# w_down loaded in whole rows, and the last expert group worked expert by expert, in a decoder block with a mixture of experts

## The chip, the core and the metric

The kernel runs on one core of a Trainium2 chip. Such a core has a matrix engine (PE in the profile, with its weight loads listed apart as PEld), a vector engine (DVE), a scalar engine (ACT), a general engine (POOL) and a sequencer that does nothing here but issue transfers (SP). Weights come from HBM, the chip's memory, through 16 DMA engines into SBUF; PE writes its sums to PSUM. The metric is the device time of one execution in microseconds (us), lower is better. Times inside a profile are counted from the start of its span, which runs from the first instruction to the last.

## The reference

One decoder block on 256 tokens of 1024 columns, all in float32: attention beside a convolution, cross-attention into a memory, and then the part that the change touches, a mixture of 32 experts and a last norm. A token picks one of 4 groups and two of its 8 experts. Cut to that:

```python
def hierarchical_moe(h, w_route_group, b_route_group, w_route_expert, b_route_expert, w_gate, w_up, w_down):
    t = h.reshape(-1, D)                                   # 256 x 1024
    ...                                                    # gates [32, 256]: two entries per token
    def expert_step(y, args):
        wg, wu, wd, ge = args                              # 1024x512, 1024x512, 512x1024
        out = (jax.nn.silu(t @ wg) * (t @ wu)) @ wd
        return y + ge[:, None] * out, None
    y, _ = lax.scan(expert_step, jnp.zeros_like(t), (w_gate, w_up, w_down, gates))

x = x + hierarchical_moe(rmsnorm(x, norm_ffn_g), ...)
return rmsnorm(x, final_g)
```

Each of `w_gate`, `w_up` and `w_down` is 2.1 MB per expert, so the 32 experts hold 201 of the 237 MB that the program moves.

## The kernel before, in words

The first third of the time goes to the norms, the attention, the convolution, the cross-attention and the routing. Then come the experts, in 8 groups of 4. An expert takes up to 32 tokens, so a group fills 128 slots. For one group:

- `gather` (L968) multiplies the tokens `X` by a matrix `SR` that picks and scales them, which gives `tg`, the tokens transposed, with the 32 slots of expert q in columns 32q to 32q+31.
- 32 products each for `eg` (gate) and `eu` (up) at L1151. Expert q uses only the 32 columns of PE that belong to it, so four experts stand side by side in the array; a product of float32 shows as two records in the trace. Each needs the weights of that expert.
- `hidden_T` (L985 to L992) makes silu(eg) * eu and transposes it into `hT`.
- 32 products `ed` (L1181) with `w_down`, in two column halves of 512, the four experts again side by side; ACT copies each half from PSUM to `yd` (L1000), and `combine` (L1002) adds it, weighted by the gates in `GST`, to the experts' sum `Y`, which stays in PSUM over all groups.

In the last group the columns come in slices of 512, 256, 128 and 128, and the products go expert after expert. Behind each slice `out_slice` adds the residual `X` (L1099), squares and sums on ACT (`fjunk`, L1102) and multiplies by the last gain (L1107); after the last slice the root (`fr`, L1104), its reciprocal (L1213), the scaling and four transfers to the output follow. ACT needs another table for the root; the kernel loads it ahead of time (L1192).

All weights go through one ring of slots of 1024 KB, called 1 MB here (1.0486 million bytes; class `Ring`). SP issues the loads in one fixed order, group by group: 8 loads of `w_gate`, 8 of `w_up`, 8 of `w_down`. A load waits until the slot that it takes has been read for the last time, and for the eighth transfer before it, since eight completion semaphores go round. `w_gate` and `w_up` are cut by rows: a partition's piece of a load is 4 rows of 512 floats that follow each other in memory, 8 KB. `w_down` is cut by columns: a partition's piece is 512 columns of each of its 4 rows, four runs of 2 KB; in the last group the runs are 2 KB, 1 KB and 512 bytes (`down_cols`). The last gain `final_g` is loaded by ACT's queue in the last group and takes its turn on those semaphores (L1163).

Of the kernel before, what the change touches and what calls it, by code (L numbers as in the profile page):

```python
# [16 lines left out]
OP = mybir.AluOpType  # L17
# [3 lines left out]
P = 128  # L21
# [37 lines left out]
class Ring:  # L59
    """Weight loads in a fixed order through slots of SBUF: a load starts as soon as a slot is free.  # L60
    Larger tensors of the first phase live in slots too, so that their memory joins as they end."""
# [25 lines left out]
    def spare(self, shape, dt=F32):  # L87
        """a slot for another tensor [P, *shape]: the tensor and the slot"""
# [9 lines left out]
    def queue(self, key, shape, src, within=None):  # L98
        """within: the load of an earlier key whose slot this one shares, and the columns there"""
        self.todo.append((key, shape, src, within))  # L100

    def pump(self, limit=1000):
        while self.todo and limit:
# [13 lines left out]
            # the very first in two parts, so that the arithmetic starts sooner  # L117
# [22 lines left out]
class Pair:  # L140
    """An operand [P, NJ, S] of 24 significant bits as two of 12; each half of its rows in one slot."""
# [16 lines left out]
def down_cols(g):  # L158
    """column slices of w_down's loads; finer at the end"""
    return [(0, 512), (512, 512)] if g < NE // 4 - 1 else [(0, 512), (512, 256), (768, 128), (896, 128)]  # L160


def body(tc, a, out):
# [55 lines left out]
    # U[s, t] = 1 where s <= t  # L219
# [3 lines left out]
    # the same in bf16, which holds 0 and 1 exactly  # L223
# [4 lines left out]
    # the tensor engine's clock rests when it idles: products nobody reads keep it up meanwhile  # L228
# [16 lines left out]
    # router columns: NG group columns, padding that never wins, NE expert columns  # L245
# [4 lines left out]
    # group of each expert column  # L250
# [18 lines left out]
    # the chunks of v and the forget gate are wider than the others  # L269
# [30 lines left out]
    for g in range(NE // 4):  # L300
# [5 lines left out]
        for n, (c0, w) in enumerate(down_cols(g)):  # L306
            for q in range(4):
                wv = w_down[4 * g + q].rearrange("(p j) n -> p j n", j=4)
                if n < 3:
                    ring.queue(("ed", g, n, q), (4, 256 if n == 2 else w), wv[:, :, c0:c0 + w])  # L310
                else:
                    ring.queue(None, (4, w), wv[:, :, c0:c0 + w], (("ed", g, 2, q), slice(128, 256)))
# [30 lines left out]
    def rsqrt(src, scale, shape, name, pool=None, out=None):  # L343
        """(src * scale + eps) ** -0.5, with one Newton step on the vector engine"""
# [17 lines left out]
    def ssq(ss, src, eng):  # L362
        """ss [P, 1] = sum of squares along src [P, n]"""
# [8 lines left out]
    def ssq_rstd(src, n, name):  # L372
        """src [P, NT, n] -> rstd [P, NT]"""
# [11 lines left out]
    def split(v):  # L385
        """hi + lo == v exactly, each of 12 significant bits; a few rows of v at a time"""
# [17 lines left out]
    def put_split(pair, j, src, g):  # L404
        """split (src * g) into pair[:, j]"""
# [3 lines left out]
    def transposed(pair, src, g, k0, k1, cols, name):  # L409
        """pair[:, k] = split of g[:, k] * (cols(k) of src)^T, for k in k0 .. k1"""  # L410
# [14 lines left out]
    def normed(src, dst):  # L425
        """rmsnorm, without the gain, of src [P, NT, D] into dst"""
# [11 lines left out]
    def wstat(key, pair, name):  # L438
        """256 columns of a projection, transposed: two [P, S] in PSUM"""
# [10 lines left out]
    def astat(key, pair, n, name, outs=None, first=True, last=True, j0=0, bank=mm_ps):  # L450
        """n columns of a projection, natural: NT tiles [P, n] in PSUM"""
# [85 lines left out]
    # log_sigmoid(f) = min(f, 0) - ln(1 + exp(-|f|)) and its cumulative sum  # L537
# [14 lines left out]
    def cum_2():  # L552
        """-c by head"""
# [6 lines left out]
    def cum_3():  # L560
        """-c the same in every partition: [masked block 0 | block 0 | masked block 1]"""
# [266 lines left out]
    def x_blocks(i, k0, k1):  # L828
        """tT[:, k] = gain * (columns of block k)^T for the tokens of tile i"""
# [24 lines left out]
    # the last products tile by tile, so that the first tile's steps run beside the second's  # L854
# [42 lines left out]
    # experts outside the token's group drop out  # L897
# [15 lines left out]
    # place of each token in its expert's list, from 1  # L913
# [20 lines left out]
    # the experts' sum, [NT][2] tiles [P, 512], grows in PSUM over all groups  # L934
    Yp = [[psY.tile([P, 512], F32, name="Y%d%d" % (i, n)) for n in range(2)] for i in range(NT)]

# [1 line left out]
    last_pick = [None]  # L938

    def pick_mats(key_v, n, eng, SR=None):  # L940
        """S picks tokens into slots; SR has 1/rms for its ones"""
# [11 lines left out]
    def gate_mats(Sv, g_v, n):  # L953
        """the gates in place of S's ones"""
# [291 lines left out]
```

## Time and profile before

| | before |
|---|---|
| time, median of 3 runs | 707.68 us (706.91 to 707.87) |
| span of the profiled execution | 705.3 us |
| PE busy | 583.4 us (83% of the span) |
| DVE, ACT, POOL busy | 32%, 25%, 17% |
| moved by DMA | 237.36 MB, 337 GB/s over the span |
| mean granted clock of PE | 0.971 of full speed |

The profile gives its execution by the span; the median of the runs is 2.4 us longer than it. A busy PE is not one at its peak, since its records overlap. From about 264 us on, the 16 DMA engines are busy without a break until about 692 us.

### The profile page before, as it was taken

How to read it: one execution, taken by the hardware profiler on the slowest of the kernel's cores; microseconds unless marked ns; L12 is line 12 of the kernel's file. 1: busy time of each engine (PE TensorE's matmuls, PEld its weight loads, DVE VectorE, ACT ScalarE, POOL GpSimd, SP SyncE). 2: the span in 40 equal slices, each digit the busy share in tenths (PEclk: the TensorE clock that was granted, in tenths of full speed). 3: DMA queues.
4: the chain of work that ended last, by engine and by line, in shares of the span. 5: the costliest groups of instructions: out<-in, count | busy, mean ns of one | idle time of the engine just before them, and what ended most of it. 6: DMA issues, size and time to landing. Idle time of an engine off the chain costs nothing. (4 is left out here: it accounts for less than half of the span.)

```text
span 705.3 us, 8963 instructions
## 1 busy us (share of the span) xinstructions
PE 583.4 (83%) x3517; PEld 344.8 (49%) x3517; DVE 224.2 (32%) x496; ACT 175.0 (25%) x384; POOL 122.1 (17%) x106
## 2 busy tenths in 40 slices
PE   7999999899899999998657856866796787679685
PEld 4999889678897752525112511511251151125124
DVE  5799789785765620401000100100010010001013
ACT  6474765484444600010000000000000000000023
POOL 5556435493434100000000000000000000000000
PEclk9999999999999999999999999998998999999898
DMA  7979630666756979999999999999999999999993
GB/s 255 358 186 367 235 112 11 228 239 234 302 172 263 339 305 419 409 390 420 418 393 407 419 409 390 421 419 392 408 417 410 390 420 419 392 407 417 413 341 117
DMA packets 91164, 237.36 MB, mean 337 GB/s; under 512 B 11996, under 2 KB 36720, under 8 KB 74736
## 3 DMA queue, kind: packets, MB, share of 16 engines
q1 hardware_dynamic: 90688, 235.72, 87.6%
q10 hardware_dynamic: 432, 1.05, 0.4%
q8 instruction: 28, 0.46, 0.3%
q14 instruction: 16, 0.13, 0.1%
HBM read 235.70 MB, written 1.05 MB: 336 GB/s over the span
## 5 line engine op out<-in xcount | busy, mean ns | idle before, releaser
L1151 PE MATMUL eu<-w,tg 128*32 128x512 f32 x512 | 100.2, 680 | 47.8 <-DMA w<-in_w_up 47.8
L396 POOL TENSOR_TENSOR WL<-w,WH 128x512 fp32r<-128x512 f32 (+1 forms) x80 | 112.2, 1414 | 112.4 <-ACT WH L394 93.0
L1181 PE MATMUL ed<-w,hT 128*32 128x512 f32 (+2 forms) x576 | 90.8, 549 | 29.3 <-DMA w<-in_w_down 23.8
L394 ACT CAST WH<-w 128x512 fp32r<-128x512 f32 (+1 forms) x120 | 72.8, 619 | 47.7 <-PE pmk L401 7.3
L1151 PEld LDWEIGHTS eu<-w,tg 128*32 128x32 f32 x512 | 21.3, 122 | 122.9 <-DMA w<-in_w_up 83.1
L950 POOL TENSOR_SCALAR SR<-S,r 128x128 f32<-128x128 f32 x7 | 4.2, 603 | 397.9 <-PE Y L1002 397.9
L1181 PEld LDWEIGHTS ed<-w,hT 128*32 128x32 f32 x576 | 25.6, 109 | 88.1 <-DMA w<-in_w_down 41.3
L986 DVE TENSOR_TENSOR sgm<-sgm,eu 128x512 f32<-128x512 f32 x8 | 5.5, 688 | 196.4 <-PE eu L1151 167.3
L968 PEld LDWEIGHTS tgp<-SR,X 128*128 128x128 f32 x256 | 61.8, 335 | 11.6 <-ACT SR L949 10.7
L968 PE MATMUL tgp<-SR,X 128*128 128x128 f32 x256 | 63.5, 410 | 4.4 <-ACT SR L949 4.4
L1151 PE MATMUL eg<-w,tg 128*32 128x512 f32 x512 | 63.0, 595 | 3.2 <-DMA w<-in_w_gate 3.2
L492 DVE SCALAR_TENSOR_TENSOR cacc<-z,pT,cacc 128x256 f32<-128x256 f32 x116 | 56.4, 486 | 2.6
L956 DVE TENSOR_TENSOR S<-S,GT 128x256 f32<-128x256 f32 x8 | 3.4, 425 | 133.9 <-POOL SR L950 133.8
L396 DVE TENSOR_TENSOR WL<-w,WH 128x512 fp32r<-128x512 f32 (+1 forms) x40 | 37.5, 938 | 15.6 <-ACT WH L394 15.5
L992 ACT COPY hT<-hTp 128x512 f32<-128x512 f32 x8 | 4.7, 585 | 149.2 <-PE hTp L989 149.2
L1000 ACT COPY yd<-ed 128x512 f32<-128x512 f32 (+2 forms) x18 | 9.7, 538 | 124.0 <-PE ed L1181 124.0
L1002 PE MATMUL Y<-yd,GST 128*128 128x512 f32 (+1 forms) x64 | 30.9, 605 | 8.5 <-ACT yd L1000 8.5
L985 ACT ACTIVATE sgm<-eg 128x512 f32<-128x512 f32 x8 | 4.8, 597 | 131.9 <-PE eg L1151 131.9
L1151 PEld LDWEIGHTS eg<-w,tg 128*32 128x32 f32 x512 | 16.3, 109 | 41.3 <-issue 32.3
L969 DVE TENSOR_TENSOR tg<-tgp,g_norm_ffn_g 128x512 f32<-128x512 f32 (+1 forms) x18 | 11.4, 633 | 53.0 <-PE tgp L968 53.0
L1002 PEld LDWEIGHTS Y<-yd,GST 128*128 128x128 f32 x64 | 10.8, 189 | 28.8 <-ACT yd L1000 21.5
L400 PE MATMUL pmk<-w,WH 128*128 128x256 f32 x64 | 18.8, 294 | 0.0
(332 smaller groups left out, 949.3 us busy)
## 6 DMA issues: line engine op xcount, KB each, us to landing
w<-in_w_up SPq DMA_DIRECT2D x64, 1024.0 KB, 19.9
w<-in_w_gate SPq DMA_DIRECT2D x64, 1024.0 KB, 14.3
w<-in_w_down SPq DMA_DIRECT2D x60, 1024.0 KB, 14.4
w<-in_w_mkv SPq DMA_DIRECT2D x8, 1024.0 KB, 13.3
w<-in_w_in SPq DMA_DIRECT2D x7, 1024.0 KB, 10.4
w<-in_w_out SPq DMA_DIRECT2D x4, 1024.0 KB, 10.8
w<-in_w_mq SPq DMA_DIRECT2D x4, 1024.0 KB, 13.2
w<-in_w_mo SPq DMA_DIRECT2D x4, 1024.0 KB, 6.1
```

What stands on the lines that cost most here:

```text
L394: A.copy(hi, src)
L396: (V if nsplit[0] % 3 == 0 else G).tensor_tensor(lo, src, hi.bitcast(F32), op=OP.subtract)
L400: T.matmul(o, L[0], R[0], start=first, stop=False)
L492: V.scalar_tensor_tensor(dst, z[:, cb, t:t + S], pT[:, 4 * t + cb:4 * t + cb + 1], acc, op0=OP.mult, op1=OP.add)
L968: T.matmul(t[:, j], X[:, i, ja + j::NJ], SR[:, i], start=i == 0, stop=i == NT - 1)
L969: V.tensor_tensor(tg[:, ja:ja + step], t, gff[:, ja:ja + step].unsqueeze(2).to_broadcast([P, step, n]), op=OP.mult)
L985: A.activation(sg, pg[0:n], AF.Silu)
L986: V.tensor_mul(sg, sg, pu[0:n])
L1000: ins = A.copy(yd[:, :w], pd[0:n, :w])
L1002: T.matmul(outs[i], GST[:, i], yd[:, :w], start=first, stop=last)
L1151: T.matmul(o[32 * q:32 * q + 32], tg[:, j, 32 * q:32 * q + 32], ws[q][0][:, jj], start=j == 0, stop=j == NJ - 1, tile_position=(0, 32 * q))
L1181: T.matmul(o[32 * q:32 * q + 32, :w], hh[:, j, 32 * q:32 * q + 32], ws[q][0][:, j, :w], start=j == 0, stop=j == 3, tile_position=(0, 32 * q))
```

## The change

- Loads of `w_down` are cut by rows: a load of 1 MB holds, for each partition, 2 whole rows of 1024 floats. There are 8 per group as before. Both column halves now accumulate at once, in two PSUM tiles, and both `combine` calls follow at the end.
- In the last group the loads are ordered by expert: 6 row loads for the experts 0 to 2, and the last expert alone in column slices of 512, 256 and 256 (`LAST_COLS`), so 9 loads in place of 16.
- `last_down` takes one expert at a time and puts four blocks of its columns side by side on PE (L1023). Each block comes out on other partitions, so four copies, two on ACT and two on DVE, bring them to the expert's rows of `yd` (L1030), and the sums into the tokens contract 64 rows, two experts, at a time (L1037).
- The gain of the first 512 output columns is multiplied on POOL, not on DVE. The preload of the root's table is written behind a product of PE, not behind a copy of ACT.

```diff
-def down_cols(g):
-    return [(0, 512), (512, 512)] if g < NE // 4 - 1 else [(0, 512), (512, 256), (768, 128), (896, 128)]
+LAST_COLS = [(0, 512), (512, 256), (768, 256)]
...
-        for n, (c0, w) in enumerate(down_cols(g)):
-            for q in range(4):
-                wv = w_down[4 * g + q].rearrange("(p j) n -> p j n", j=4)
-                if n < 3:
-                    ring.queue(("ed", g, n, q), (4, 256 if n == 2 else w), wv[:, :, c0:c0 + w])
...
+        last = g == NE // 4 - 1
+        order = [(h, q) for h in range(2) for q in range(4)]
+        if last:
+            order = [(h, q) for q in range(3) for h in range(2)]
+        for h, q in order:
+            wv = w_down[4 * g + q].rearrange("(p j) n -> p j n", j=4)
+            ring.queue(("ed", g, h, q), (2, D), wv[:, 2 * h:2 * h + 2, :])
+        if last:
+            wv = w_down[NE - 1].rearrange("(p j) n -> p j n", j=4)
+            for n, (c0, w) in enumerate(LAST_COLS):
+                key = None if n == 2 else ("el", n)
+                ring.queue(key, (4, 512), wv[:, :, c0:c0 + w], (("el", 1), slice(256, 512)) if n == 2 else None)
...
+    def last_down(hh, GST, yd):
+        def down(q, w, rows, c0, o):
+            m = o.shape[1]
+            for jj, j in enumerate(rows):
+                for c in range(4):
+                    T.matmul(o[32 * c:32 * c + 32], hh[:, j, 32 * q:32 * q + 32], w[:, jj, c0 + m * c:c0 + m * c + m],
+                             start=j == 0, stop=j == 3, tile_position=(0, 32 * c))
+        def to_rows(q, o, c0):
+            m = o.shape[1]
+            for c in range(4):
+                dst = yd[32 * q:32 * q + 32, c0 + m * c:c0 + m * c + m]
+                (A.copy if c % 2 == 0 else V.tensor_copy)(dst, o[32 * c:32 * c + 32])
+        def to_tokens(q0, c0, outs, first, last=True):
+            r = slice(32 * q0, 32 * q0 + 64)
+            for i in range(NT):
+                w = outs[i].shape[1]
+                ins = T.matmul(outs[i], GST[r, i], yd[r, c0:c0 + w], start=first, stop=last)
+            return ins
+        for q in range(3):
+            o = e_ps("ed", (P, 256))
+            for h in range(2):
+                w, pool = ring.take(("ed", NGR - 1, h, q))
+                down(q, w, (2 * h, 2 * h + 1), 0, o)
+                ring.done(pool)
+            to_rows(q, o, 0)
+            if q == 1:
+                for n in range(2):
+                    ins = to_tokens(0, 512 * n, Ycols(512 * n, 512), False, n == 1)
+                with tc.issue_after(ins.ins):
+                    A.preload_act_table(AF.Sqrt)
+                for i in range(NT):
+                    V.tensor_add(X[:, i, 512:], Yp[i][1], X[:, i, 512:])
+        for n, (c0, m) in enumerate(LAST_COLS):
+            ...
+            down(3, w, range(4), 256 if end else 0, o)
+            to_rows(3, o, c0)
+            ...
+            to_tokens(2, c0, outs, n > 0)
+            ...
+            out_slice(n, c0, m, outs, X, end)
...
-                V.tensor_mul(Z[:, i, cs], Z[:, i, cs], fin["g"][:, cs])
+                (V if n else G).tensor_tensor(Z[:, i, cs], Z[:, i, cs], fin["g"][:, cs], op=OP.mult)
...
+        if not last:
+            os_ = [e_ps("ed") for _ in range(2)]
+            for h in range(2):
+                ws = [ring.take(("ed", g, h, q)) for q in range(4)]
+                for jj in range(2):
+                    j = 2 * h + jj
+                    for n in range(2):
+                        for q in range(4):
+                            T.matmul(os_[n][32 * q:32 * q + 32], hh[:, j, 32 * q:32 * q + 32],
+                                     ws[q][0][:, jj, 512 * n:512 * n + 512],
+                                     start=j == 0, stop=j == 3, tile_position=(0, 32 * q))
...
+            for n in range(2):
+                combine(os_[n], P, GST, yd[:, n], Ycols(512 * n, 512), 512, g == 0)
+        else:
+            last_down(hh, GST, yd.rearrange("p n w -> p (n w)"))
```

A scheduler orders the instructions of each engine, so the diff does not tell all. Three places in the built programs follow; `L` is the line in the kernel's file, and x8 stands for eight such instructions in a row.

SP, the loads from the end of group 6 to the end of the last group (7), before. A shape of 128x2048 is one run of 8 KB per partition, 128x4x512 is four runs of 2 KB:

```order
L121 DMA w<-in_w_down 128x4x512 x8
L121 DMA w<-in_w_gate 128x2048 x8
L121 DMA w<-in_w_up 128x2048 x8
L121 DMA w<-in_w_down 128x4x512 x4
L121 DMA w<-in_w_down 128x4x256 x4
L121 DMA w<-in_w_down 128x4x128 x8
```

The same place in the changed program:

```order
L121 DMA w<-in_w_down 128x2048 x8
L121 DMA w<-in_w_gate 128x2048 x8
L121 DMA w<-in_w_up 128x2048 x8
L121 DMA w<-in_w_down 128x2048 x6
L121 DMA w<-in_w_down 128x4x512
L121 DMA w<-in_w_down 128x4x256 x2
```

Every load of `w_down` outside the last expert now has the shape of a load of `w_gate`.

PE, the end of the program, before (`yl` are the sums of the last column slices):

```order
L1181 MATMUL ed<-w,hT 32x256 x14
L1181 MATMUL ed<-w,hT 32x128 x4
L1002 MATMUL Y_3091<-yd,GST 128x256
L1002 MATMUL Y_3093<-yd,GST 128x256
L1181 MATMUL ed<-w,hT 32x128 x12
L1002 MATMUL yl<-yd,GST 128x128 x2
L1181 MATMUL ed<-w,hT 32x128 x16
L1002 MATMUL yl<-yd,GST 128x128 x2
```

PE, the end of the changed program:

```order
L1023 MATMUL ed<-w,hT 32x256 x10
L1023 MATMUL ed<-w,hT 32x128 x16
L1023 MATMUL ed<-w,hT 32x64 x16
L1037 MATMUL yl<-yd,GST 128x256
L1037 MATMUL Y_3090<-yd,GST 128x512
L1037 MATMUL Y_3092<-yd,GST 128x512
L1037 MATMUL yl<-yd,GST 128x256
L1023 MATMUL ed<-w,hT 32x64 x16
L1037 MATMUL yl<-yd,GST 128x256 x2
```

The sums of the first 512 columns (`Y_3090`, `Y_3092`) now stand behind the products of the second slice and ahead of those of the last.

ACT, the end of the program, before:

```order
L1000 COPY yd<-ed 128x512
L1192 ACT_TABLE_LOAD
L1102 ACTIVATE fjunk,fss<-w 128x512 x2
L1000 COPY yd<-ed 128x256
L1102 ACTIVATE fjunk,fss<-w 128x256
L1000 COPY yd<-ed 128x128
L1102 ACTIVATE fjunk,fss<-w 128x256
L1102 ACTIVATE fjunk,fss<-w 128x128 x2
L1000 COPY yd<-ed 128x128
L1102 ACTIVATE fjunk,fss<-w 128x128
L1104 ACTIVATE fr<-fss,fpart 128x1
```

ACT, the end of the changed program:

```order
L1030 COPY yd<-ed 32x128
L1030 COPY yd<-ed 32x64 x2
L1030 COPY yd<-ed 32x128
L1168 ACTIVATE fjunk,fss<-w 128x512 x2
L1030 COPY yd<-ed 32x64
L1168 ACTIVATE fjunk,fss<-w 128x256
L1030 COPY yd<-ed 32x64
L1168 ACTIVATE fjunk,fss<-w 128x256 x2
L1170 ACT_TABLE_LOAD
L1170 ACTIVATE fr<-fss,fpart 128x1
```

The table load has moved from behind the first copy to directly ahead of the first root, and the two copies of the last slice stand behind the squares of the first 512 columns.

## Rows read from the trace of the kernel before

**Rows 1.** The page: DMA throughput in 40 equal slices of the span.

```profile
GB/s 255 358 186 367 235 112 11 228 239 234 302 172 263 339 305 419 409 390 420 418 393 407 419 409 390 421 419 392 408 417 410 390 420 419 392 407 417 413 341 117
```

**Rows 2.** DMA view: packets of 300 to 312 us, then of 320 to 332 us.

```profile
DMA packets 2319, 4.63 MB, mean 386 GB/s; under 512 B 64, under 2 KB 64, under 8 KB 2318
...
DMA packets 688, 5.01 MB, mean 418 GB/s; under 512 B 77, under 2 KB 77, under 8 KB 77
```

**Rows 3.** Stretches: from:to, length, busy PE, PEld, DVE, ACT, POOL, PEclk, DMA share, GB/s.

```profile
247.00:256.00 9.00, 8.82 (x54) 5.65 (x52) 2.67 (x10) 0.40 (x1) 0.00 (x0) 1.00 0.60 235
264.00:290.00 26.00, 23.32 (x154) 10.21 (x147) 6.50 (x21) 2.16 (x4) 0.61 (x1) 0.97 1.02 421
...
480.00:496.00 16.00, 11.78 (x62) 2.95 (x63) 0.69 (x1) 0.58 (x1) 0.00 (x0) 0.79 1.04 386
505.00:525.00 20.00, 18.19 (x110) 10.68 (x106) 2.48 (x5) 0.99 (x2) 0.60 (x1) 0.91 1.01 419
```

**Rows 4.** Order of time, SP: start, length, what, how many; first loads of groups 2, 3.

```profile
306.53 12.17 SPq L121 DMA_DIRECT2D w<-in_w_gate  x8
...
368.08 12.15 SPq L121 DMA_DIRECT2D w<-in_w_gate  x8
```

**Rows 5.** Order of time, PE: group 0's first gate products; gathers for groups 1, 2.

```profile
251.60 3.64 PE L1151 MATMUL eg<-w,tg 128*32 128x512 f32 x32
...
285.61 7.89 PE L968 MATMUL tgp<-SR,X 128*128 128x128 f32 x32 [0.82 <-ACT SR L949]
...
325.20 7.91 PE L968 MATMUL tgp<-SR,X 128*128 128x128 f32 x32 [0.57 <-ACT SR L949]
```

**Rows 6.** The chain that ended last: its first piece and a late one.

```profile
674.80 8.91 PE ed L1181 x34
...
694.56 2.40 PE ed L1181 x32
```

**Rows 7.** Stretches in the last group, columns as in rows 3.

```profile
669.00:677.00 8.00, 6.39 (x38) 1.97 (x32) 0.69 (x1) 0.58 (x1) 0.00 (x0) 1.00 1.05 385
679.00:681.50 2.50, 2.50 (x14) 0.78 (x11) 0.00 (x0) 0.00 (x0) 0.00 (x0) 1.00 1.09 350
...
692.00:700.00 8.00, 5.31 (x62) 4.46 (x59) 3.94 (x17) 3.70 (x17) 0.00 (x0) 1.00 0.00 1
```

**Rows 8.** Order of time, PE and DVE, last group; in brackets the idle time before.

```profile
642.53 4.49 PE L1151 MATMUL eg<-w,tg 128*32 128x512 f32 x38
...
668.81 3.62 PE L1151 MATMUL eu<-w,tg 128*32 128x512 f32 x26 [1.47 <-DMA w<-in_w_up]
...
690.44 1.13 PE L1002 MATMUL Y<-yd,GST 128*128 128x256 f32 x4 [0.42 <-ACT yd L1000]
691.18 0.42 DVE L1099 TENSOR_TENSOR w<-Y,X 128x256 f32<-128x256 f32 x1 [2.57 <-PE Y L1002]
...
694.49 2.46 PE L1181 MATMUL ed<-w,hT 128*32 128x128 f32 x32
```

**Rows 9.** Order of time, ACT: a table load early on, and the last steps.

```profile
39.44 1.28 ACT L519 ACT_TABLE_LOAD   x1
40.73 0.63 ACT L394 CAST WH<-w 128x520 fp32r<-128x520 f32 x1
...
686.31 0.63 ACT L1102 ACTIVATE fjunk<-w 128x512 bf16<-128x512 f32 x1 [0.70 <-DVE w L1099]
686.84 0.18 ACT L1102 ACTIVATION_READ_ACCUMULATOR fjunk<-w 128x1 f32 x1
...
696.99 0.27 ACT L1000 COPY yd<-ed 128x128 f32<-128x128 f32 x1 [1.29 <-PE ed L1181]
...
698.22 0.31 ACT L1102 ACTIVATE fjunk<-w 128x128 bf16<-128x128 f32 x1 [0.96 <-DVE fpart L1199]
...
701.10 0.34 ACTq L1218 DMA_DIRECT2D out_dram<-w  x1
```

**Rows 10.** SP's own waits between 600 and 700 us: total, times, longest.

```profile
SPq L121 <- DMA w<-in_final_g: 11.4, 1, 11.4
```

More of the change, by code (lines that the diff above doesn't have):

```diff
@@ L935, in body @@
     Yp = [[psY.tile([P, 512], F32, name="Y%d%d" % (i, n)) for n in range(2)] for i in range(NT)]
+    NGR = NE // 4
     last_pick = [None]
@@ L1006, in Ycols @@
         return [Yp[i][c0 // 512][:, c0 % 512:c0 % 512 + w] for i in range(NT)]
+    def last_down(hh, GST, yd):
[31 more added lines that the diff above has]
+        for n, (c0, m) in enumerate(LAST_COLS):
+            if n < 2:
+                w, pool = ring.take(("el", n))
+            end = n == 2
+            o = e_ps("ed", (P, m // 4))
+            down(3, w, range(4), 256 if end else 0, o)
+            to_rows(3, o, c0)
+            if n == 0:
+                outs = Ycols(0, 512)
+            else:
+                outs = [e_ps("yl", (P, m)) for _ in range(NT)]
+            to_tokens(2, c0, outs, n > 0)
+            if end:
+                V.tensor_reduce(fin["part"], fin["ss"][:, :, 0:n], AX.X, OP.add)
+                V.tensor_scalar(fin["part"], fin["part"], 1.0 / D, EPS, op0=OP.mult, op1=OP.add)
+            out_slice(n, c0, m, outs, X, end)
+            if n != 1:
+                ring.done(pool)
@@ L1137, in body @@
     state = (tg0, gate_mats(S0, quad(GT, 0), P))
-    NGR = NE // 4
     table = None
@@ L1169, in body @@
         yd = new_yd(P)
-        for n, (c0, w) in enumerate(down_cols(g)):
-            o = e_ps("ed")
-            if n < 3:
-                ws = [ring.take(("ed", g, n, q)) for q in range(4)]
-            else:
-                ws = [(v[:, :, 128:], pool) for v, pool in ws]
-            order = [(j, q) for j in range(4) for q in range(4)]
-            if last:
-                order = [(j, q) for q in range(4) for j in range(4)]
-            for j, q in order:
-                T.matmul(o[32 * q:32 * q + 32, :w], hh[:, j, 32 * q:32 * q + 32], ws[q][0][:, j, :w],
-                         start=j == 0, stop=j == 3, tile_position=(0, 32 * q))
-            if n != 2:
+        if not last:
[9 more added lines that the diff above has]
+                                     start=j == 0, stop=j == 3, tile_position=(0, 32 * q))
@@ L1184, in body @@
                 for q in range(4):
                     ring.done(ws[q][1])
-            end = last and n == len(down_cols(g)) - 1
-            if n < 2:
-                outs = Ycols(c0, w)
-                ins = combine(o, P, GST, yd[:, n % 2], outs, w, g == 0, last)
-                if last and n == 0:
-                    with tc.issue_after(ins.ins):
-                        A.preload_act_table(AF.Sqrt)
-            else:
-                for i in range(NT):
-                    V.tensor_add(X[:, i, c0:c0 + w], Ycols(c0, w)[i], X[:, i, c0:c0 + w])
-                if end:
-                    V.tensor_reduce(fin["part"], fin["ss"][:, :, 0:n], AX.X, OP.add)
-                    V.tensor_scalar(fin["part"], fin["part"], 1.0 / D, EPS, op0=OP.mult, op1=OP.add)
-                outs = [e_ps("yl", (P, w)) for _ in range(NT)]
-                combine(o, P, GST, yd[:, n % 2], outs, w, True, True)
@@ L1202, in body @@
-            if last:
-                out_slice(n, c0, w, outs, X, end)
+            for n in range(2):
+                combine(os_[n], P, GST, yd[:, n], Ycols(512 * n, 512), 512, g == 0)
+        else:
+            last_down(hh, GST, yd.rearrange("p n w -> p (n w)"))
         if g == 0:
@@ L1210, in body @@
     ov_ = out[0].rearrange("(i p) d -> p i d", p=P)
-    h, c0 = D // 2, D - 128
+    h, c0 = D // 2, LAST_COLS[-1][0]
     for i in range(NT):
```

2 lines of the change are left out of this document (removed).

## The prediction

> **What bounds the kernel now.** I read the page's throughput first, then stretches of the stage, then the chain of waits. The page shows low and uneven rates for the first third and then a regular pattern: two or three slices near 420 GB/s, one or two near 390 [rows 1]. The DMA view says what the two levels are. At 300 to 312 us nearly all packets are under 8 KB, 4.63 MB in 2319 packets, 2 KB each: `w_down`. At 320 to 332 us 611 of 688 packets are 8 KB and more: `w_gate` and `w_up` [rows 2]. By stretches the first kind runs at 386 GB/s and the second at 419 to 421, with the DMA share at 1.01 to 1.04 in both [rows 3]. So the DMA engines are full and the packet size goes with the rate. The order of time on SP gives the period: the first load of group 2 is issued at 306.53, that of group 3 at 368.08, 61.55 us later [rows 4]. That is the sum of the two rates: a group has 16 loads at 1.0486/0.4195 = 2.50 us and 8 at 1.0486/0.386 = 2.717, 61.7 us. PE alone would need less: while the weights of group 1 were nearly all there, it took 325.20 - 285.61 = 39.6 us from one gather to the next [rows 5]. From group 1 to group 7 the weight stream is the bound.
>
> At the very end it is not. The chain that ended last begins at 674.80 with the first `ed` products of group 7 and stays on PE and the engines behind it without one transfer [rows 6]. The last weights are in by 692, where throughput falls to 1 GB/s [rows 7], yet PE begins the last 32 records only at 694.49 [rows 8]. So there are two accounts: the stream up to the last `w_up` load, and the tail from there, which PE, ACT and DVE share.
>
> **The stream.** Every load of `w_down` outside the last expert takes the shape of a gate load: one run of 8 KB per partition, 16 KB from one partition's to the next. The same run, pitch, queue and slot as gate loads, so I take their rate. Groups 1 to 6 hold 48 such loads: 48 x (2.717 - 2.50) = **10.4 us** less. With the rows' least and most favourable rates (386, against 418 to 421 [rows 2, 3]) it is 10.0 to 10.8.
>
> Group 0 I put at nothing. Its `w_down` is in before the stream is full: at 247 to 256 us the DMA share is 0.60 [rows 3], because the next slots come free only when the first gate products have been read, 251.60 to 255.24 [rows 5]. PE and routing set that moment. Faster loads only make that gap longer. Were it not so, 8 loads would give 8 x 0.217 = 1.7 us: bounds 0 to 1.7.
>
> A shorter period needs cover elsewhere. Both `combine` calls now follow the last `ed` product, which puts one pair of `Y` products, 2 x 0.86 us (256 columns take half of it, below), behind the last load of a group and delays the next gather by 1.7 us. The 59.8 us period against 39.6 us of PE work hides it. It is queued ahead of the next gate products, whose slots are freed that much later; but SP then still has up to eight loads, 20 us, in flight.
>
> On this the Trainium skill, page "DMA: Bandwidth & Descriptors", section "Specifications", speaks against the change: from 512 bytes on a transfer is at line rate, which would make 2 KB as good as 8 KB. By that rule the 10.4 would be 0; the rows of 386 and 419 GB/s contradict it as long as the packet size is their cause, and 2 KB and 8 KB differ by 8.5% here.
>
> **The tail.** Let t0 be 668.81, when the last `w_up` load lets PE go on [rows 8]; all of the tail moves with it. Before, the first square of the last slice starts at t0 + 29.4 (698.22) and the last output transfer is issued at t0 + 32.3 (701.10) [rows 9]. The change, step by step:
>
> Weights: 6 row loads at 2.50, one of 2 KB runs 2.72, and two halves of 1 KB runs at 350 GB/s [rows 7], 1.5 each. They land at t0 + 15.0, 17.7, 19.2 and 20.7. Before, they ended near 692, t0 + 23.2: so the weights come 2.5 us sooner, but PE is what counts.
>
> Products: 16 of 64 columns per slice, four blocks side by side, 32 records. Side by side, 38 records of 512 columns took 4.49 us, 0.118 each; one after another, 32 records of 128 columns took 2.46 [rows 8]. Bounds for a slice: 0.118/8 x 32 = 0.5 and 2.46; I take 1.4, in between, since the tiles are side by side but very short. The second slice is through at 19.2 + 1.4 = 20.6.
>
> Copies: four per slice, two per engine; a copy of twice the width and four times the partitions took 0.27 [rows 9], so at most 0.5, to 21.0.
>
> Then PE has, in its order, `yl` of 256 columns, two `Y` of 512 and `yl` of 256 ahead of the last slice. Four records of 256 columns took 1.13, and the first result was used 0.74 after their start [rows 8]: 0.43 for 256 columns, 0.86 for 512, plus 0.3 until a result can be used. That is 2.6 us, to 23.6, with the two `Y` ready at 22.6 and 23.4. The last slice, landed at 20.7, runs 23.6 to 25.0. Contracting 64 rows may cost the full price or half; I take the full one, that of the row.
>
> ACT has two squares of 512 columns, some 0.8 each with their sums (0.63 alone [rows 9]), ahead of the last copies; with 0.7 for the add on DVE (0.42 for half the columns [rows 8]) they run 23.3 to 25.0. Copies and one more square go to 26.0, `yl` to 26.8. DVE has a gain product, behind a square that ends at 26.6, ahead of the last add: 0.42 + 0.15 + 0.42. So the last square starts at **t0 + 27.7**, 1.7 earlier than before.
>
> Against that, the square has 256 columns (+0.1) and the table load now stands between it and the root: 1.28 us [rows 9], no longer under PE's work. The rest of the end keeps its 2.9 us, +0.1 for wider pieces. The last transfer goes at 27.7 + 2.9 + 1.5 = t0 + 32.1, against 32.3: **-0.2 us**. The POOL products are done long before, since its 512-column products need some 3 us from t0 + 24.
>
> The Trainium skill, page "ScalarE: Activation LUTs", section "What ACT_TABLE_LOAD costs", adds a drain of 1.38 us to such a load; the one at 39.44 took 1.28 and the next instruction began at 40.73 [rows 9], so no drain shows there. By the page the tail would be +1.2.
>
> Bounds: with blocks at 0.5 and half-price sums the last square starts about 1.5 sooner, -1.7. With blocks at 2.46 twice, +2.1; and PE's clock may fall, as it did at 480 to 496 us, granted 0.79 on the mean, in a stage where PE waits for loads [rows 3]. At 1.2 GHz the 5.4 us of PE from the second slice on would double; half of it +2.7. Together at most about +4.
>
> **Sum.** 705.3 - 10.4 - 0.2 = 694.7 us of span; what lies around it, 2.4 us to the median of the runs, stays: **697.1 us**.
>
> **The rivals.**
>
> A, the tail costs: low clock, serial blocks or a dearer table load, +1.5 to +4. For it: PE now waits for each expert, as in the `w_up` stretches that precede low clocks. Against: some of these waits are ahead of work that waits anyway. Price: 697.1 + 3 = 700.
>
> B, the tail gains as well: cheap sums and blocks, -1.7, or group 0 saves its 1.7 too. 695.
>
> C, the stream gains nothing: the lower rate belongs to `w_down` as such, not to its packets, the page's rule in this kernel. Against: the same tensor's 1 KB pieces run at 350, so the rate follows the size [rows 7]. 707.5, no change.
>
> D, slower: `final_g`. In the last group the tenth load, the second of `w_up`, shares its semaphore with `final_g` and waits until that has landed. Before, SP stood 11.4 us for it [rows 10] and throughput held, since the loads ahead kept the engines fed. Now 7 loads are ahead, 17.5 us. Every microsecond beyond that is lost; it decides from 10.4 + 0.2 + 1.4 = 12 us of empty queue. ACT now issues it ahead of the group's `SR`, not behind it, so sooner. It would give 709 and more.
>
> **Chances.** 0.72 for the forecast, its own range 696 to 698.8; A 0.14, B 0.08, C 0.04, D 0.02. From 694.8, B, to 701, most of A, lie at least 8 in 10. The runs of this kernel spread 0.14%, so 0.2%, 1.4 us, is what a measurement can tell from no change. Forecast, A and B are all faster by more: 0.94; within it C and a rest, 0.04; slower D, 0.02.
>
> **What would show it.** Right: period between first gate loads near 59.8 us in groups 2 to 6; no stretch near 386 GB/s until the last expert; the last `w_up` lands near 658; from there 32 us to the last transfer issue; a table load of 1.28 us directly ahead of the first root; PE waits longer for loads than before. Wrong: stretches under 410 GB/s with packets of 8 KB (C); a DMA share well under 1 around 640 us (D); PEclk under 0.8 behind the last `w_up` (A); a period near 59.8 but a first stage of other length, which nothing here accounts for.

## The result, and the profile after

The changed kernel takes **700.6 us** (median of 8 runs, 699.6 to 705.1) against 707.7 before; the ratio is 0.989, with a 95% interval of 0.986 to 0.992. The forecast was 697.1, with a range of 694.8 to 701.0. So the sign and the main term were right, and 3.5 us of the forecast gain are missing: the forecast's own range, 696 to 698.8, was missed, and the time is the one that rival A had (700). The profiled execution took 699.7 us with a span of 698.0, where 694.7 was forecast.

The page of the changed kernel, throughput in 40 equal slices, to be held against [rows 1]:

```profile
GB/s 251 358 184 366 214 155 1 240 216 209 303 170 256 339 290 421 420 419 419 419 421 419 420 419 421 418 423 418 420 419 421 419 419 420 420 419 418 421 336 62
```

From the 16th slice on it is flat near 420; the slices at 390 are gone. Stretches, with the columns of [rows 3] (the first holds `w_down` of group 1, the next lies where `w_down` was at 386 before):

```profile
300.00:316.00 16.00, 13.86 (x111) 4.35 (x104) 0.69 (x1) 1.10 (x2) 0.00 (x0) 1.00 1.02 421
480.00:496.00 16.00, 12.69 (x59) 3.36 (x52) 0.69 (x1) 0.59 (x1) 0.00 (x0) 1.00 1.01 421
505.00:525.00 20.00, 17.63 (x104) 10.81 (x102) 2.47 (x5) 1.00 (x2) 0.60 (x1) 1.00 1.01 419
```

Order of time on SP, the first loads of `w_down` of group 0 and of `w_gate` of groups 2, 3 and 7, beside [rows 4]:

```profile
225.34 19.30 SPq L121 DMA_DIRECT2D w<-in_w_down  x8
...
299.90 17.80 SPq L121 DMA_DIRECT2D w<-in_w_gate  x8
...
360.11 17.78 SPq L121 DMA_DIRECT2D w<-in_w_gate  x8
...
600.98 20.28 SPq L121 DMA_DIRECT2D w<-in_w_gate  x8
```

Before, the first and the last of these rows stood at 224.37 and 615.84:

```profile
224.37 19.72 SPq L121 DMA_DIRECT2D w<-in_w_down  x8
...
615.84 14.62 SPq L121 DMA_DIRECT2D w<-in_w_gate  x8
```

The first period, from group 2 to 3, is 60.21 us, where it was 61.55. Over the five periods to group 7 it is 60.22 on the mean (301.08 in all), where it was 61.86 (309.31). That is 1.65 us less per group, 9.9 for six groups, and 1.73 per group were forecast.

Order of time on PE of the changed kernel, the last group, beside [rows 8]:

```profile
659.61 3.62 PE L1216 MATMUL eu<-w,tg 128*32 128x512 f32 x26 [1.45 <-DMA w<-in_w_up]
...
665.59 1.93 PE L1023 MATMUL ed<-w,hT 128*32 128x256 f32 x32 [0.77 <-ACTq L1119]
670.59 4.18 PE L1023 MATMUL ed<-w,hT 128*32 128x256 f32 x44 [3.07 <-issue]
674.70 3.94 PE L1037 MATMUL Y<-yd,GST 64*128 64x512 f32 x8
678.58 2.81 PE L1023 MATMUL ed<-w,hT 128*32 128x256 f32 x84
682.62 0.67 PE L1037 MATMUL yl<-yd,GST 64*128 64x256 f32 x2 [1.24 <-DVE yd L1030]
...
685.37 0.65 PE L1023 MATMUL ed<-w,hT 128*32 128x64 f32 x32
```

t0, the last `w_up` load, is 659.61. Before, from 224.37 to t0 it took 444.44 us, now from 225.34 to t0 434.27: **the stream and what hangs on it gave 10.2 us**. The stretch ahead of it is 0.97 longer, and behind t0 there is something new: PE stops for 3.07 us after 32 records, for nothing that the profile names ("issue"). The end on ACT, and one expert's copies on ACT and then on DVE:

```profile
667.63 0.36 ACT L1030 COPY yd<-ed 32x256 f32<-32x256 f32 x1 [2.19 <-PE ed L1023]
668.47 0.36 ACT L1030 COPY yd<-ed 32x256 f32<-32x256 f32 x1 [0.48 <-DVE yd L1030]
...
689.50 0.42 ACT L1168 ACTIVATE fjunk<-w 128x256 bf16<-128x256 f32 x1 [1.43 <-DVE fpart L1069]
...
690.03 1.28 ACT L1170 ACT_TABLE_LOAD   x1
691.33 0.29 ACT L1170 ACTIVATE fr<-fss,fpart 128x1 f32<-128x1 f32 x1
...
693.88 0.35 ACTq L1266 DMA_DIRECT2D out_dram<-w  x1
...
668.02 0.41 DVE L1030 COPY yd<-ed 32x256 f32<-32x256 f32 x1 [4.01 <-ACT yd L1030]
668.87 0.42 DVE L1030 COPY yd<-ed 32x256 f32<-32x256 f32 x1 [0.43 <-ACT yd L1030]
```

The last square starts at t0 + 29.9 and the last transfer is issued at t0 + 34.3; before it was 29.4 and 32.3 [rows 9]. **The tail costs 2.0 us.** With +0.97 - 10.17 + 1.98 the change is -7.2, which is what the spans show (705.3 to 698.0). Against the forecast span that is 2.2 us in the tail, 1.0 ahead of the stream and 0.2 in the stream. Three marks stand in these rows: the stop, the copies that take turns (each waits for the other engine's, 1.65 us for four), and the table load right ahead of the root.

The 0.97 us ahead of the stream are PE's clock. In the changed kernel's profile:

```profile
13.10:16.40 3.30, 3.30 (x18) 3.30 (x17) 2.27 (x4) 2.27 (x6) 1.44 (x2) 0.50 0.78 236
```

The granted clock (third number from the end) is 0.50, 1.2 GHz, over this stretch; in the profile of before the first 100 us have 1.00. It isn't the change: the profiles below, whose first stage is the same code, start `w_down` of group 0 at 224.1 to 229.1.

### The profile page after: what moved, and what is told of

Its sections match the earlier page's. It is cut to its first block, busy times and chain, and to the rows that moved or that the text cites. A ratio compares the mean times of both kernels' runs of the same rounds, so it can differ in the third digit from the quotient of the medians.

```text
span 698.0 us, 9091 instructions
## 1 busy us (share of the span) xinstructions
PE 595.1 (85%) x3585; PEld 352.8 (51%) x3585; DVE 227.3 (33%) x500; ACT 176.6 (25%) x388; POOL 124.6 (18%) x108
## 5 line engine op out<-in xcount | busy, mean ns | idle before, releaser
L1243 PE MATMUL ed<-w,hT 128*32 128x512 f32 x448 | 91.4, 598 | 17.4 <-DMA w<-in_w_down 12.6
L975 PEld LDWEIGHTS tgp<-SR,X 128*128 128x128 f32 x256 | 61.9, 335 | 10.8 <-ACT SR L956 10.0
L1243 PEld LDWEIGHTS ed<-w,hT 128*32 128x32 f32 x448 | 21.9, 109 | 81.8 <-issue 40.4
L1216 PE MATMUL eg<-w,tg 128*32 128x512 f32 x512 | 61.6, 595 | 0.9 <-DMA w<-in_w_gate 0.9
L1216 PEld LDWEIGHTS eg<-w,tg 128*32 128x32 f32 x512 | 17.9, 109 | 35.9 <-issue 27.9
L1007 ACT COPY yd<-ed 128x512 f32<-128x512 f32 x14 | 8.2, 586 | 100.7 <-PE ed L1243 100.7
L1009 PE MATMUL Y<-yd,GST 128*128 128x512 f32 x56 | 25.9, 605 | 0.0
L406 PE MATMUL pmk<-w,WH 128*128 128x256 f32 x64 | 18.8, 294 | 0.0
L407 PE MATMUL pmk<-w,WH 128*128 128x256 f32 x64 | 18.5, 290 | 0.0
## 6 DMA issues: line engine op xcount, KB each, us to landing
w<-in_w_in SPq DMA_DIRECT2D x7, 1024.0 KB, 10.4
```

The source lines that it names most:

```text
L406: T.matmul(o, L[0], R[0], start=first, stop=False)
L407: T.matmul(o, L[0], R[1], start=False, stop=False)
L975: T.matmul(t[:, j], X[:, i, ja + j::NJ], SR[:, i], start=i == 0, stop=i == NT - 1)
L1007: ins = A.copy(yd[:, :w], pd[0:n, :w])
L1009: T.matmul(outs[i], GST[:, i], yd[:, :w], start=first, stop=last)
L1216: T.matmul(o[32 * q:32 * q + 32], tg[:, j, 32 * q:32 * q + 32], ws[q][0][:, jj], start=j == 0, stop=j == NJ - 1, tile_position=(0, 32 * q))
```

## Experiments

Ratios are to the kernel before, run on the same chip; "tail" is t0 to the last output transfer of the one profiled execution. A star marks profiles in which PE's clock was low while the last 26 `eu` records ran (5.3 to 6.6 us for them in place of 3.62), so the tail holds 1.7 us (`table_early` 2.95) that the last group's code doesn't make. In `table_early` and `tail_only` the clock was low near the end as well (the last 32 `ed` records took 1.08 us in place of 0.65), so their tails hold something more of that kind.

| kernel | median us | ratio, 95% | tail us |
|---|---|---|---|
| before | 707.7 | | 32.3 |
| changed | 700.6 | 0.989 (0.986 to 0.992) | 34.3 |
| rows_only | 696.9 | 0.985 (0.981 to 0.988) | 32.4 |
| tail_only | 710.6 | 1.003 (1.001 to 1.006) | 35.3 |
| rows_4k | 700.6 | 0.990 (0.989 to 0.991) | 32.3 |
| table_early | 699.2 | 0.987 (0.984 to 0.990) | 35.5* |
| copies_free | 699.6 | 0.987 (0.984 to 0.990) | 35.2* |
| pad20 | 703.5, one run | | 37.8* |
| pad45 | 702.7 | 0.991 (0.989 to 0.993) | 38.5 |
| all_pad | 701.9 | 0.990 (0.987 to 0.993) | 36.5 |
| warm | 696.1 | 0.980 (0.977 to 0.984) | 31.8* |
| best | 694.1 | 0.978 (0.975 to 0.981) | 30.9* |
| fill_pad | 696.9 | 0.984 (0.980 to 0.987) | 32.2 |
| fill_only | 702.8 | 0.990 (0.987 to 0.993) | 37.1 |

### The two halves of the change, each alone

`rows_only` is before with this for groups 0 to 6, and the changed kernel's loop over them:

```diff
+        if g < NE // 4 - 1:
+            for h in range(2):
+                for q in range(4):
+                    wv = w_down[4 * g + q].rearrange("(p j) n -> p j n", j=4)
+                    ring.queue(("ed", g, h, q), (2, D), wv[:, 2 * h:2 * h + 2, :])
+            continue
```

> The kernel before with one part of the change: in groups 0 to 6 w_down comes in whole rows and both combines follow at the end; the last group stays as before, in column slices of all four experts. My theory: the gain of the change comes from the stream alone (10.4 us in groups 1 to 6), and the new last group costs 2 us. Then this kernel is faster than the changed one: 707.7 - 10.4 = 697.3 us, 696.5 to 698.6, with the last transfer issued 32.3 us behind the last w_up load, as before. Rival: the last group is 2 us longer because the weights now come sooner and in another phase, whatever its products look like. Then it gives about 700.6, the time of the changed kernel.

`tail_only` is the changed kernel with the opposite:

```diff
-            ring.queue(("ed", g, h, q), (2, D), wv[:, 2 * h:2 * h + 2, :])
+            if last:
+                ring.queue(("ed", g, h, q), (2, D), wv[:, 2 * h:2 * h + 2, :])
+            else:
+                ring.queue(("ed", g, h, q), (4, 512), wv[:, :, 512 * h:512 * h + 512])
```

> The changed kernel with w_down of groups 0 to 6 back in column halves: only the new last group remains (six row loads, then the last expert in column slices, blocks side by side). My theory: slower than before by the 2 us of the last group, 709.7 us (708.5 to 710.5), last transfer 34.3 us behind the last w_up load. Rival: the last group saves as the forecast said or costs nothing by itself: 707.5.

696.9 and 710.6 us: the row loads alone are worth 10.8 us, and the new last group alone costs 2.8 by the medians on that chip, 0.1 above its expected range, and 2.3 by the ratio (its interval, 0.1% to 0.6%, holds the 2.0 as well). Row loads with the old last group are the better kernel: the changed one is 3.7 us slower by the medians, though the two intervals overlap by a little. The rival, that any last group would be longer behind the faster stream, is out: in `rows_only` the tail is what it was. Order of time, PE and the last transfer:

```profile
658.39 3.62 PE L1157 MATMUL eu<-w,tg 128*32 128x512 f32 x26 [1.48 <-DMA w<-in_w_up]
...
690.74 0.34 ACTq L1239 DMA_DIRECT2D out_dram<-w  x1
```

In `tail_only` the stop of the changed kernel is there again, with 3.33 us:

```profile
680.78 4.59 PE L1026 MATMUL ed<-w,hT 128*32 128x256 f32 x46 [3.33 <-issue]
```

### What makes the row loads faster

```diff
-                    ring.queue(("ed", g, h, q), (2, D), wv[:, 2 * h:2 * h + 2, :])
+                    ring.queue(("ed", g, h, q), (2, D), wv[:, h::2, :])
```

> The kernel with row loads alone (last group as before), but a load takes rows 0 and 2 or rows 1 and 3 of a partition's four, so the runs in memory are 4 KB and not 8. Theory: a packet costs a fixed part and one by its bytes. From 2 KB at 386 and 8 KB at 420 GB/s over 16 engines (85 and 312 ns each) the fixed part is 9 ns and the rest goes at 27 GB/s; 4 KB then take 161 ns, 408 GB/s, and 48 loads are 3.5 us slower than in rows of 8 KB: 700.4 us (699.3 to 701.2). Rival: what helps is that a load takes whole rows; then it stays at 696.9. Second rival: everything below 8 KB goes at the low rate; then the gain is gone, 707.

700.6 us. A stretch of `w_down` in group 1 of `rows_4k`, and the DMA view of the same 12 us:

```profile
302.00:314.00 12.00, 10.37 (x82) 3.38 (x76) 0.69 (x1) 0.59 (x1) 0.00 (x0) 0.86 1.03 410
```

```profile
DMA packets 1277, 4.92 MB, mean 410 GB/s; under 512 B 77, under 2 KB 77, under 8 KB 1277
```

1277 packets, all but 77 of 4 KB, at 410 GB/s: the law of a fixed 9 ns per packet plus its bytes at 27 GB/s per engine said 408. For 1 KB, which it was not fitted to either, it gives 349, and [rows 7] have 350. Both rivals are out: whole rows don't help by themselves (3.6 us are lost against `rows_only`, and the intervals of the two lie apart), and below 8 KB there is no single low rate.

### The three marks of the tail

`table_early` loads the root's table behind ACT's second copy of the second expert (`cp`); `copies_free` spreads the four blocks over two PSUM tiles, so that ACT and DVE read different ones:

```diff
-                with tc.issue_after(ins.ins):
+                with tc.issue_after(cp.ins):
                     A.preload_act_table(AF.Sqrt)
```

> The changed kernel with one edit: the root's table is loaded behind an ACT copy of the second expert, where ACT waits for PE, and no longer directly ahead of the root. My theory: the 1.28 us of that load lie on the path that ends last, so 700.6 - 1.3 = 699.3 us (699.0 to 699.7). Rival: the load hides behind something else that ends as late (the sums of squares, DVE's part), then 700.3 to 700.6.

```diff
-                    T.matmul(o[32 * c:32 * c + 32], hh[:, j, 32 * q:32 * q + 32], w[:, jj, c0 + m * c:c0 + m * c + m],
+                    T.matmul(o[c % 2][32 * c:32 * c + 32], hh[:, j, 32 * q:32 * q + 32], w[:, jj, c0 + m * c:c0 + m * c + m],
...
-            o = e_ps("ed", (P, 256))
+            o = [e_ps("ed", (P, 256)) for _ in range(2)]
```

> The changed kernel with one edit: the four column blocks of a slice come out in two PSUM tiles, blocks 0 and 2 (copied by ACT) in one, 1 and 3 (copied by DVE) in the other, so that no copy has to wait for one of the other engine. My theory: the copies of one slice take 0.9 in place of 1.65 us, and as those of the third expert and of the last one's slices stand in the chain of the last group, the end moves by 0.8 to 2 us: 698.6 to 699.8. Rival: PE and the order of the squares set the end, and the copies are hidden: 700.3 to 700.9.

699.2 and 699.6 us, both in the range of my theory, but neither is told apart from the change by its interval, so the 1.4 and 1.1 us are not shown. What the second edit does is plain in the order of time, ACT and then DVE: two copies each with no wait between, 0.9 us for all four in place of 1.65.

```profile
672.41 0.74 ACT L1030 COPY yd<-ed 32x256 f32<-32x256 f32 x2 [2.21 <-PE ed L1023]
...
672.47 0.86 DVE L1030 COPY yd<-ed 32x256 f32<-32x256 f32 x2 [3.70 <-PE ed L1023]
```

### The stop of PE

During the stop, the DMA view of the changed kernel from 667 to 670 us shows, among 163 packets of weights, one of 16 KB that holds instructions:

```profile
DMA packets 165, 1.23 MB, mean 410 GB/s; under 512 B 16, under 2 KB 16, under 8 KB 16
...
q8 instruction: 1, 0.02, 2.2%
```

Just ahead PE has jumped over the path for overflowing experts. So I shifted where the jump lands, with products that nobody reads, 20 in `pad20` and 45 in `pad45`:

```diff
+        if g == 5:
+            t = e_ps("pad")
+            for _ in range(20):
+                T.matmul(t[:, 0:64], onesb, onesb[:, 0:64], start=True, stop=True)
```

> The changed kernel with 20 small products that nobody reads (bf16, 64 columns, 40 instructions with their weight loads) ahead of group 5 on PE, where PE waits for weights anyway. In the changed kernel PE stops for 3.1 us after 32 ed records of the last group, for nothing that the profile names, while 16 KB of instructions come in over the DMA engines. My theory: PE jumps over the overflow path into the middle of a block of instructions, runs out of it after some 70, and waits for the next block. 40 more instructions ahead of the jump leave it 30: the stop comes after 10 to 14 records and not after 32, and ends at about the same distance from the jump, some 5.5 us. Rival: PE waits for something of the second expert (its weights, a buffer, a copy); then the stop stays behind the 32nd record.

> As the run with 20 small products, with 45 (90 instructions), which is more than the 70 that are left in the block. My theory: the jump now lands at the start of a block, the stop behind record 32 is gone, the second expert is worked when its loads land, and the last group is 1.5 to 2 us shorter: 699.0 us (698.6 to 699.8). It could also be that the block is not there yet at the jump; then the stop of some 3 us moves to the jump, ahead of the first ed product, and the time stays near 700.6. Rival (a wait for the second expert): the stop stays where it is and so does the time, 700.6.

`pad20`, order of time on PE: the stop comes after 13 records, and ends 4.96 us behind the first of them, as in the changed kernel (5.00).

```profile
667.54 1.06 PE L1023 MATMUL ed<-w,hT 128*32 128x256 f32 x13 [0.82 <-ACTq L1119]
672.50 5.78 PE L1023 MATMUL ed<-w,hT 128*32 128x256 f32 x63 [3.90 <-issue]
```

19 records fewer are, with the weight load of each, 38 instructions, for 40 put in. **The stop is a wait for instructions**, shown by moving it. In `pad45` it is gone, and yet the time is 702.7 us, not 699:

```profile
664.46 2.80 PE L1023 MATMUL ed<-w,hT 128*32 128x256 f32 x48 [0.77 <-ACTq L1119]
...
672.88 7.19 PE L1037 MATMUL Y<-yd,GST 64*128 64x512 f32 x8
680.00 4.99 PE L1023 MATMUL ed<-w,hT 128*32 128x256 f32 x84
```

```profile
671.00:684.00 13.00, 12.97 (x78) 5.82 (x80) 2.05 (x4) 0.69 (x2) 0.00 (x0) 0.50 0.48 171
```

The second fence is the stretch: a granted clock of 0.50 over 13 us. Without the stop PE works each half as it lands and waits in between, and the clock then falls just where its work is on the path: eight `Y` records take 7.19 us (3.94 in the changed kernel), the next 84 4.99 (2.81). In this profile the tail is 38.5 us, 4.2 longer than with the stop; by the medians, whose intervals overlap, nothing was gained. My expectation had left the clock out.

### All edits, and PE kept busy

> The changed kernel with three edits together: the root's table loaded early, the blocks in two PSUM tiles so that copies don't wait for each other, and the 45 small products. My theory: the table's 1.3, the copies' 1.1 and what the stop behind record 32 costs (0 to 2) add up: 696.0 to 698.3 us, against 700.6 of the change and 696.9 of the row loads alone. Rival: they overlap, or the landing of the last slice sets the end; then it stops at about 698.5.

701.9, above the range and the rival alike: the clock is at 0.50 in the same place, and of the three gains nothing is left. `warm` puts products into the waits; they write the third expert's tile (`bank(2)`) before its own products start:

```diff
+        def fill(o, n):
+            for _ in range(n):
+                T.matmul(o[0], hh[:, 0], hh[:, 0:2].rearrange("p j n -> p (j n)"), start=True, stop=True)
...
+                if (q, h) in ((1, 1), (2, 0)):
+                    fill(bank(2), 3)
```

> The run with all three edits, and beside them six products that nobody reads (float32, 256 columns, 0.43 us each) where PE waits for the second and third expert of the last group. In the run without them PE's granted clock was 0.5 from 670.7 to 684.4, right behind those waits, and eight Y records took 7.19 in place of 3.7 us, the next 86 of ed 4.9 in place of 2.8. My theory: what the shorter waits gave was lost to the clock; with PE busy in between the clock stays and the last group is 5 us shorter: 696.3 us (695.5 to 697.5). Rival: the clock falls in any case or something else takes those 5 us; then it stays at 701 to 702.

696.1, as expected. The stretch that was at 0.50, and the `Y` records in it:

```profile
671.00:684.00 13.00, 12.98 (x146) 7.41 (x137) 3.92 (x8) 3.49 (x8) 0.00 (x0) 1.00 0.82 304
```

```profile
676.85 3.70 PE L1041 MATMUL Y<-yd,GST 64*128 64x512 f32 x8
```

`best` goes on from there:

```diff
-                ins = (A.copy if c % 2 == 0 else V.tensor_copy)(dst, o[c % 2][32 * c:32 * c + 32])
+                ins = (A.copy if c % 2 == 0 and c0 < LAST_COLS[2][0] else V.tensor_copy)(dst, o[c % 2][32 * c:32 * c + 32])
...
-            else:
-                (V if n else G).tensor_tensor(Z[:, i, cs], Z[:, i, cs], fin["g"][:, cs], op=OP.mult)
+            elif n == 0:
+                G.tensor_tensor(Z[:, i, cs], Z[:, i, cs], fin["g"][:, cs], op=OP.mult)
...
-        V.tensor_scalar(Z[:, i, h:c0], Z[:, i, h:c0], r[:, i:i + 1], None, op0=OP.mult)
-        V.scalar_tensor_tensor(Z[:, i, c0:], Z[:, i, c0:], r[:, i:i + 1], fin["g"][:, c0:], op0=OP.mult, op1=OP.mult)
+        V.scalar_tensor_tensor(Z[:, i, h:], Z[:, i, h:], r[:, i:i + 1], fin["g"][:, h:], op0=OP.mult, op1=OP.mult)
```

> As the run with the six products, with two edits at the very end: all four copies of the last slice on DVE, since ACT's two stood behind its squares (0.5 us after DVE's), and no gain product of 256 columns on DVE, which took 0.89 each beside POOL's product; the gain of the last 512 columns goes into the last scaling, one instruction of 512 columns in place of two of 256. My theory: both stand in the chain ahead of the last square, 1.2 us together: 695.1 us (694.2 to 696.3), below the row loads alone (696.9). Rival: the squares on ACT set the end anyway; then it equals the run with the six products.

694.1 us, 0.1 under its range and the fastest of all: 2.2% below before, where the changed kernel is 1.1% below, and the two intervals lie apart. Against `rows_only` they just meet.

Last, the share of stop and clock alone, without the early table and the free copies:

> The changed kernel with the 45 small products ahead of group 5 (no stop behind record 32) and the six products that nobody reads between the experts, but with the table load and the copies as in the change. My theory, if the parts add up: all edits gave 696.1, the early table 1.4 and the free copies 1.1 of it, so this one gives 698.6 us (697.7 to 699.5): 2.0 below the change, and 4 below the run with the 45 products alone (702.7), which is the price of the clock. Rival: most of the 4.5 us that all edits gave come from stop and clock and the other two don't add up with them: 697 or less.

> The same without the 45 products: the stop of 3 us behind record 32 is still there, and the six products stand between the experts. My theory: PE still loses the 3 us, and the clock may still fall behind it, so little is gained over the change: 699.3 to 700.8 us. Rival: the stop is hidden by the wait for the loads, and keeping PE busy is all that counts: then it equals the run with both, 698.6.

696.9 and 702.8. In the last group of `fill_pad` there is no stop, and the clock is low only in the very last four products (2.07 us in place of 1.13, from 684.42 on), which DVE's work hides; order of time on PE, DVE and ACT:

```profile
658.55 3.62 PE L1233 MATMUL eu<-w,tg 128*32 128x512 f32 x26 [1.46 <-DMA w<-in_w_up]
...
671.31 3.70 PE L1037 MATMUL Y<-yd,GST 64*128 64x512 f32 x8
...
684.17 1.54 DVE L1186 TENSOR_TENSOR w<-w 128x256 f32<-128x256 f32 x2 [0.76 <-ACT fjunk L1181]
...
686.33 0.42 ACT L1181 ACTIVATE fjunk<-w 128x256 bf16<-128x256 f32 x1 [1.43 <-DVE fpart L1082]
...
690.71 0.35 ACTq L1283 DMA_DIRECT2D out_dram<-w  x1
```

Its tail is 2.1 shorter than the changed kernel's, as my theory had it, and `warm`'s again shorter (31.8 less 1.7 is 30.1); its median, though, is what the rival said. Medians of six runs with clocks that differ from run to run don't settle whether the parts add up. `fill_only` missed on the other side: the products stand behind the stop, the first three of them run at the low clock (0.51 from 675.3 to 678.3 us) and delay the second expert:

```profile
674.38 1.07 PE L1023 MATMUL ed<-w,hT 128*32 128x256 f32 x16 [3.23 <-issue]
675.38 2.93 PE L1042 MATMUL ed<-hT 128*128 128x256 f32 x6
```

Six records of theirs take 2.93 us there; in `fill_pad` 1.56. Between the two kernels, which differ by the 45 products alone, lie 5.9 us.

## Why the prediction was right, and where its tail failed

**The stream** was right in mechanism and size: 10.4 forecast, 10.2 between the first `w_down` load and t0, 10.8 by `rows_only`. `w_down` runs at 421 where it was at 386, with DMA engines full in both. Rival C is out by this, and `rows_4k` shows the cause to be the size of the packet. The Trainium skill, page "DMA: Bandwidth & Descriptors", section "Specifications", has 512 bytes as enough for line rate; by it the change would have given nothing. The runs contradict it: 386, 410 and 421 GB/s at 2, 4 and 8 KB of the same tensor. The Trainium skill, page "Perfetto Trace Analysis", section "DMA Optimizations", speaks for batching small transfers into larger ones, 2 KB into 4 or 8 KB, and has a dramatic gain possible. The runs agree on the direction; here, where a load is 1 MB in any case and only its packets grow, the gain is 6% and 9%.

**Group 0 at nothing** fits too: at 247 to 256 us the changed kernel moves 281 GB/s at a DMA share of 0.67, so the gap ahead of the full stream is still there, and B's gain from it did not come.

```profile
247.00:256.00 9.00, 8.76 (x56) 5.31 (x55) 3.54 (x15) 1.18 (x2) 0.00 (x0) 1.00 0.67 281
```

**The first stage** was 0.97 us longer in this profile. The text named it as what nothing accounts for; it is PE's clock, and chance. The 2.4 us around the span were in part chance too: the runs lasted 1.6 to 1.8 us longer than their spans, and the rest is how far the profiled one lay from the median, some 0.7 before and 0.9 now.

**The tail** is the step that failed: "-0.2 us", from a last square at t0 + 27.7 and a last transfer at t0 + 32.1. It came at 29.9 and 34.3. Where PE isn't stopped and keeps its clock, the forecast times are met: `fill_pad` has them at t0 + 27.8 and 32.2. To 0.1 us that is luck, since sizes in the working were off in opposite directions. 32 records of the last slice take 0.65 us, not 1.4 (row 685.37, near the lower bound). The copies, put at 0.5 at most for a slice, hold the next product up for 1.24 (row 682.62), since four copies share a PSUM tile and take turns. And the two gain products on DVE ahead of the last add take 1.54 in `fill_pad` and 1.55 in the changed kernel, where the working had one of 0.42. The full price for 64 rows was right (four `Y` records of 64 rows took 1.88 us in the changed kernel, with 128 rows before 1.98), and so was the table load, 1.28, with 0.02 to the next instruction: no drain.

What was missing is the jump: the working has no term for it, and so puts the fetch of instructions behind it at nothing. In the kernel before, a packet of instructions came in as well, between 677 and 678 us, some 3 us behind the first `ed` record, but there PE had 8.8 us of slow products in hand and did not stop:

```profile
674.80 8.83 PE L1181 MATMUL ed<-w,hT 128*32 128x512 f32 x36 [0.78 <-ACTq L1053]
```

```profile
q8 instruction: 1, 0.02, 7.0%
```

The new products take 1.93 us per expert, so PE is done before the instructions are there. I read this as a cover that the change itself removed: the same fetch, no longer behind work. Where the jump of the kernel before lands in its block, no run shows. The Trainium skill, page "Runtime: NRT & Kernel Launch", section "Instruction fetch mechanics", has instructions arrive in blocks of 256, fetched in sequence while the engine works, and broken by a jump. The packet of 16 KB and the 90 instructions that remove the stop agree; that crossing a block is mostly hidden doesn't hold here, where PE stood for 3.1 to 3.9 us.

By its mechanism the outcome is rival A, in a form that I had not listed: +2.0 us in the tail. The clock, which I had named in A, is the other part: it fell to 0.50 right behind the stop (671.9 to 675.2 us of the changed kernel), and for 13 us when the stop alone was removed. The first of these lines is that stretch; the second is from `table_early`, where PE stopped for 3.34 us and the clock did not fall:

```profile
671.90:675.20 3.30, 3.30 (x25) 1.81 (x18) 0.84 (x2) 0.73 (x2) 0.00 (x0) 0.50 1.02 378
```

```profile
672.42 2.78 PE L1023 MATMUL ed<-w,hT 128*32 128x256 f32 x44 [3.34 <-issue]
```

The 44 records behind the stop took 4.18 us in the changed kernel and 2.78 here, and the eight `Y` records 3.94 in place of 3.70. By this estimate 1.6 of the 2.1 us that the tail is longer than in `fill_pad` are the clock, and some 0.5 are left for the stop itself, part of which would have been a wait for loads.

**D**, `final_g`, did not come: SP waited 6.5 us for it and the stretches around hold 418 to 422 GB/s. SP's waits between 600 and 700 us, beside [rows 10]:

```profile
SPq L121 <- DMA w<-in_final_g: 6.5, 1, 6.5
```

## What to carry to other kernels

When a stream of weights is the bound, count its bytes per contiguous run: the price of a load was (bytes / 27 GB/s + 9 ns per packet) per engine, and a loop order that accepts whole rows cost nothing here, where PE had slack. When work at the end is made shorter, ask what its length had covered: here, by my reading, a fetch of instructions behind a jump, and PE's clock, which fell when short work left waits in between. Two engines that copy from one PSUM tile may take turns; give each its own.

## What the runs showed of the hardware

- Throughput by run length, one core, 16 engines full: 350 GB/s at 1 KB [rows 7], 386 at 2 KB, 410 at 4 KB, 421 at 8 KB.
- Some 64 instructions behind a jump (32 records and their weight loads) PE stopped for 3.07 us while 16 KB of instructions arrived among the weights. 40 more instructions ahead of the jump brought the stop 38 instructions forward (3.90 us), and 90 more removed it.
- Filling PE's waits with products that nobody reads moved the granted clock from 0.50 to 1.00 over 13 us, and was worth 5.8 us by the medians (`all_pad` to `warm`).
- Four products of 32 columns of PE side by side, each with 64 moving columns: 32 records in 0.65 us, 0.02 each.
